# Twelve dot products of the third tile ahead of the end of the second tile's first block

## The chip, the core and the metric

The kernel runs on one core of one Trainium2 chip. The metric is the device time of one execution in microseconds (us); three executions were timed, and one was profiled. The engines are called PE (TensorE matmuls), PEld (its weight loads), DVE (VectorE), ACT (ScalarE), POOL (GpSimd) and SP (SyncE, which here only starts transfers).

## The reference

Two transformer stages over 512 tokens of width 1024, in float32. The first block mixes tokens (a convolution and an RWKV recurrence) and then has a feed-forward part made of 16,384 single-row experts: for every token 128 experts are picked (8 heads, 16 each), and

```
ue = jnp.take(expert_u, expert, axis=0)                 # 128 rows of 1024 per token
ve = jnp.take(expert_v, expert, axis=0)
h = gelu(einsum('thkd,td->thk', ue, xc))                # 128 dot products per token
return einsum('thk,thkd->td', gate * h, ve)             # weighted sum of 128 rows
```

Its result is added to the residual stream, and an RMS norm with `final_g` ends the first block. The second block has two layers (differential attention, an MLP, latent attention, a second MLP) and a last norm. Attention in it is causal.

## The kernel before

The 512 tokens are four tiles of 128 (tile 0 to 3; the change speaks of tile 1, the second, and tile 2, the third). For each tile `peer(t)` (line 980) does the expert part in two halves. The **dots** (`dots_rows`, 942): 128 times, POOL starts a gather of 128 rows of `peer_u` (one row of 4 KB per partition, so 0.5 MB), and DVE multiplies it with the tile's activations and sums along the row (line 952). The product itself goes to a scratch tile `scr`, named `dots`, that is never read; only the sum in `hc` counts. The **mix** (`mix_pe`, 957): 128 times, POOL gathers 128 rows of `peer_v`, and PE adds them with weights into one PSUM tile `pv` (line 977); the trace holds eight records for each such row set. Below, a "row" of the mix is one such gather with its matmuls.

Gathers rotate over the buffers of `k.rings`: four with the tag `gath` and four with `gatv`, for tile 2 two more with the tags `h2` and `h3`. All gathers are issued by POOL, in one order.

`x2(t)` (987) ends the first block of a tile: it loads the residual `xq` (a `gatv` buffer) and the gain `fing` (a `gath` buffer), scales `pv` and adds (1002, 1003), writes the sum to DRAM and reads it back in row layout into `h[t]`, squares it on ACT with a row sum (1009) and finishes the norm on DVE (`rstd2`, then 1013). The squares need somewhere to go as well:

```
scr = self.gp.tile([P, D], BF16, name="dots")            # dots_rows, 949
sq = self.gp.tile([P, D], BF16, name="sqr", tag="dots")  # x2, 998
```

The pool `gp` has one buffer per tag unless more are asked for, so `scr` and `sq` are one piece of memory. A tile holds its buffer until its last access; who asks next for the same tag waits for that.

The tile framework orders each engine's instructions by itself: what comes first in the program has priority, an instruction is placed when its data and its buffers are there, and later work fills what is left. The program order around the change is: `peer(1)`; the rest of the first block for tiles 1 to 3 and the routing of tiles 2 and 3; `x2(1)`; then for tile 2 and for tile 3 `peer(t)` and `x2(t)`; then the second block, which takes tiles 0 and 1 together (attention 1154, `mlp` 1233, `mla` 1271, `mlp`), then the attention of tile 2 alone, then the attention of tile 3 alone, and last `mlp`, `mla`, `mlp` for tiles 2 and 3 together. The second block's weights come in 0.5 MB tiles that ACT and DVE split into a high and a low part (211, 212). The second block of tiles 0 and 1 needs `h[0]` and `h[1]`; the transposes at its head (`norm_T`, line 1081) take both tiles into one PSUM tile, and one ACT instruction (1086) reads the pair. So in time the second block of tiles 0 and 1 runs beside the expert part of tiles 2 and 3.

Of the kernel before, what the change touches and what calls it, by code (L numbers as in the profile page):

```python
# [145 lines left out]
class K:  # L146
# [792 lines left out]
        self.gather(g, self.A[table], col)  # L939
        return g  # L940

    def dots_rows(self, t, idx):

        nc = self.nc
        if t >= 2:
            self.u2[t] = self.gp.tile([P, D], F32, name="u2", bufs=1)
            nc.sync.dma_start(self.u2[t], self.u2d[t])
        hc = self.gp.tile([P, P], F32, name="hc", bufs=1)
        scr = self.gp.tile([P, D], BF16, name="dots")
        for s in range(P):  # L950
            g = self.row('peer_u', idx[:, s:s + 1])
            self.last_dot = nc.vector.scalar_tensor_tensor(scr, g, 1.0, self.u2[t], op0=OP.mult, op1=OP.mult, accum_out=hc[:, s:s + 1])  # L952
        return hc
# [23 lines left out]
            self.nc.tensor.matmul(ps[32 * c:32 * c + 32, q, :], self.win[k // 16 % 2][:, o:o + 32], g[:, c * 256:(c + 1) * 256],  # L977
                                  start=i == 0, stop=i == 31)

    def peer(self, t, gate, idx, idxT):  # L980

        hc = self.dots_rows(t, idx)
        self.nc.scalar.activation(hc, hc, AF.Gelu)
        self.nc.vector.tensor_tensor(hc, hc, gate, op=OP.mult)
        return self.mix_pe(hc, idxT)
# [385 lines left out]
def build(tc, A, out):  # L1371
    with ExitStack() as ctx:
        k = K(tc, A, out)
# [3 lines left out]
        with ExitStack() as c1:  # L1377
            k.s1_setup(c1)
            cdots = cpeer.enter_context(ExitStack())
            routed = k.routed  # L1380

            def peer(t):
                return k.peer(t, *routed[t])
# [35 lines left out]
            *x1, conv_in = k.s1_in(g1, act1, (1, 2, 3))  # L1419
            conv_in()  # L1420
            y = peer(0)
            x = k.gp.tile([P, D], F32, name="xo", tag="gath", bufs=NGATH)
            k.x2(0, y, x)
# [10 lines left out]
            with tc.tile_pool(name="o1", bufs=1) as o1:  # L1434
                act = act_tile(o1, 1)
                k.s1_out((mix[0][:, :, :P], None), (1,), act)
                routed[1], = k.route(act, (1,), o1)
            y = peer(1)
            rwkv(2)
            rwkv(3)  # L1440
# [1 line left out]
            k.s1_out((mix[0][:, :, P:], None), (2, 3), act)  # L1442
            routed[2], routed[3] = k.route(act, (2, 3), k.rp)
        k.b2_setup(ctx)
        k.x2(1, y, k.h[1])
        cdots.close()
        tc.nc.sync.dma_start(k.h[0], k.x2d)
        g, v = k.rings[:2]
# [1 line left out]
        rings = {2: ring + [(k.b2c, "h2", 1), (k.b2c, "h3", 1)], 3: ring + [(k.b2c, "h3", 1)]}  # L1450
        for t in (2, 3):
            k.rings = rings[t]
            y = k.peer(t, *routed[t])
            k.h[t] = k.b2c.tile([P, D], F32, name=f"h{t}")
            k.x2(t, y, k.h[t])
        pool = ctx.enter_context(tc.tile_pool(name="b2", bufs=1))
# [34 lines left out]
```

## Time and profile before

| | |
|---|---|
| time of three runs | 2903.47, 2909.51 (median), 2913.26 us |
| the profiled execution | 2908.32 us, of which the profile's span is 2906.5 |
| PE busy | 2324.7 us (80% of the span) |
| DVE busy | 2036.6 us (70%) |
| POOL busy | 1239.5 us (43%) |
| ACT busy | 936.6 us (32%) |
| gathers (POOL queue) | 536.94 of 862.51 MB moved |

Busy shares are means over stages with different limits, so the stages are read one by one below. A PE share near 1 says that matmuls follow each other, not that each runs at its best speed; PEclk is the clock that the chip granted, 1.00 for 2.4 GHz and 0.50 for 1.2 GHz.

### The profile page before, as it was taken

Reading aid. Unit: us, or ns where it says so; the run is one execution under the profiler, and the core shown is the slowest. Engines: PE = TensorE matmul, PEld = TensorE weight load, DVE = VectorE, ACT = ScalarE, POOL = GpSimd, SP = SyncE. Lnnn points to the kernel's source line nnn. Section 1 sums busy time; section 2 is a strip of 40 time slices with the busy share of each in tenths; the row PEclk is TensorE's granted clock in tenths of the full one; section 3 lists DMA queues with packets and bytes.
Section 4 is the critical chain, followed back from the end, with each engine's and each line's share of the span. In section 5 each row is a group of like instructions: output and inputs, shape, how many; then the busy total and the mean of one; then the engine's idle time right before and its main releaser. Section 6 shows DMA issues by size and latency. Waiting matters only on the chain.

```text
span 2906.5 us, 50631 instructions
## 1 busy us (share of the span) xinstructions
PE 2324.7 (80%) x19212; PEld 1673.5 (58%) x19212; DVE 2036.6 (70%) x4923; ACT 936.6 (32%) x1814; POOL 1239.5 (43%) x1072
## 2 busy tenths in 40 slices
PE   6486397889672776486699997999897589999998
PEld 5365255436551541264566665778552268887897
DVE  5938987745899980599934469999751476675566
ACT  3342131031200110143333344444450255455454
POOL 0553665664376657556654434455547100000000
PEclk9668698689766886695799998999997699999999
DMA  9558898899899999998999988899999745652564
GB/s 322 168 184 318 307 402 289 290 346 348 256 360 374 399 379 409 332 350 295 365 398 363 357 290 324 297 367 384 373 369 381 258 126 182 189 157 84 157 186 135
DMA packets 249084, 862.51 MB, mean 297 GB/s; under 512 B 27652, under 2 KB 38404, under 8 KB 248840
## 3 DMA queue, kind: packets, MB, share of 16 engines
q0 software_dynamic: 147456, 536.94, 49.6%
q1 hardware_dynamic: 98792, 318.14, 32.2%
q10 hardware_dynamic: 2592, 4.20, 0.4%
q8 instruction: 151, 2.47, 0.4%
q14 instruction: 93, 0.76, 0.1%
HBM read 851.30 MB, written 7.86 MB: 296 GB/s over the span
## 4 chain that ended last, share of the span: by engine, by line
PE 35%; DVE 12%; issue 7%; DMA 3%; ACT 2%; POOL 1%; DVEq 0%; ACTq 0%; POOLq 0%
PE acc L222 9%; PE acc L223 9%; PE acc L221 9%; DVE dots L952 4%; PE pv L977 3%; DVE wlo L212 3%; DMA gath<-in_peer_v_dram,idxT 3%; PE sc L1065 2%; PE sc L1330 1%; ACT whi L211 1%; POOL gath L932 1%; PE o_ps L1342 1%; PE aT_ps L1142 1%; PE sc L1135 0%; DVE act L1087 0%
## 5 line engine op out<-in xcount | busy, mean ns | idle before, releaser
L932 POOL DMA_INDIRECT gath<-in_peer_u_dram,idx x512 | 612.1, 1195 | 511.2 <-DVE dots L952 158.9
L932 POOL DMA_INDIRECT gath<-in_peer_v_dram,idxT x512 | 544.8, 1064 | 404.7 <-PE pv L977 278.9
L212 DVE TENSOR_TENSOR wlo<-wraw,whi 128x1024 fp32r<-128x1024 f32 (+3 forms) x406 | 484.9, 1196 | 280.4 <-ACT whi L211 277.4
L952 DVE SCALAR_TENSOR_TENSOR dots<-gath,u 128x1024 bf16<-128x1024 f32 x512 | 622.7, 1216 | 20.5 <-DMA gath<-in_peer_u_dram,idx 16.9
L211 ACT ACTIVATE whi<-wraw 128x1024 fp32r<-128x1024 f32 (+3 forms) x406 | 419.9, 1036 | 510.1 <-PE acc L223 341.5
L977 PE MATMUL pv<-gath,win 128*32 128x256 f32 x4096 | 363.6, 449 | 97.7 <-DMA gath<-in_peer_v_dram,idxT 95.1
L222 PE MATMUL acc<-wlo,act 128*128 128x512 f32 (+2 forms) x924 | 375.3, 407 | 24.9 <-DVE wlo L212 23.9
L221 PE MATMUL acc<-whi,act 128*128 128x512 f32 (+2 forms) x924 | 344.8, 403 | 22.5 <-DVE qr L1115 10.2
L223 PE MATMUL acc<-whi,act 128*128 128x512 f32 (+2 forms) x924 | 361.2, 393 | 0.9 <-DVE act L200 0.8
L221 PE MATMUL acc<-act,whi 128*128 128x256 f32 x1104 | 320.1, 291 | 12.2 <-ACT whi L211 7.8
L223 PE MATMUL acc<-act,wlo 128*128 128x256 f32 x1104 | 318.4, 291 | 7.8 <-DVE wlo L212 7.4
L222 PE MATMUL acc<-act,whi 128*128 128x256 f32 x1104 | 316.6, 287 | 0.0
L219 PE MATMUL acc<-act,wraw 128*128 128x128 f32 (+2 forms) x1472 | 293.2, 357 | 4.3 <-ACT sc L856 2.7
L977 PEld LDWEIGHTS pv<-gath,win 128*32 128x32 f32 x4096 | 96.3, 116 | 286.4 <-DMA gath<-in_peer_v_dram,idxT 206.6
L219 PEld LDWEIGHTS acc<-act,wraw 128*128 128x128 f32 x1472 | 224.4, 201 | 59.4 <-issue 3.4
L222 PEld LDWEIGHTS acc<-wlo,act 128*128 128x128 f32 x924 | 176.9, 192 | 98.1 <-DVE wlo L212 50.1
L221 PEld LDWEIGHTS acc<-act,whi 128*128 128x128 f32 x1104 | 214.5, 195 | 27.7 <-ACT whi L211 10.9
L223 PEld LDWEIGHTS acc<-act,wlo 128*128 128x128 f32 x1104 | 213.9, 195 | 24.2 <-DVE wlo L212 12.2
L222 PEld LDWEIGHTS acc<-act,whi 128*128 128x128 f32 x1104 | 215.1, 195 | 4.0 <-issue 3.3
L221 PEld LDWEIGHTS acc<-whi,act 128*128 128x128 f32 x924 | 173.5, 192 | 76.0 <-issue 20.4
L223 PEld LDWEIGHTS acc<-whi,act 128*128 128x128 f32 x924 | 176.9, 192 | 34.6 <-DVE act L247 1.5
L1002 DVE TENSOR_TENSOR pv<-pv,gt_ffn 128x512 f32<-128x512 f32 x8 | 5.6, 696 | 173.8 <-PE pv L977 173.7
(422 smaller groups left out, 3132.8 us busy)
## 6 DMA issues: line engine op xcount, KB each, us to landing
wraw<-in_w_up_dram SPq DMA_DIRECT2D x128, 512.0 KB
wraw<-in_w_down_dram SPq DMA_DIRECT2D x128, 512.0 KB
wraw<-in_w_qkv_dram SPq DMA_DIRECT2D x72, 512.0 KB
wraw<-in_ada_w_dram SPq DMA_DIRECT2D x48, 512.0 KB
wraw<-in_w_q_dram SPq DMA_DIRECT2D x48, 512.0 KB
wraw<-in_w_in_dram SPq DMA_DIRECT2D x44, 512.0 KB
wraw<-in_w_out_dram SPq DMA_DIRECT2D x24, 512.0 KB
wraw<-in_w_o_a_dram SPq DMA_DIRECT2D x24, 512.0 KB
```

What stands on the lines that cost most here:

```text
L211: self.nc.scalar.activation(hi[:, :n], raw[:, :n], AF.Copy)
L212: self.nc.vector.tensor_tensor(lo[:, :n], raw[:, :n], hi[:, :n].bitcast(F32), op=OP.subtract)
L219: mm(out, l[0], r[0], start=start, stop=stop)
L221: mm(out, l[0], r[0], start=start, stop=False)
L222: mm(out, l[0], r[1], start=False, stop=False)
L223: mm(out, l[1], r[0], start=False, stop=stop)
L932: self.nc.gpsimd.indirect_dma_start(out=out, out_offset=None, in_=table, in_offset=bass.IndirectOffsetOnAxis(ap=col, axis=0))
L952: self.last_dot = nc.vector.scalar_tensor_tensor(scr, g, 1.0, self.u2[t], op0=OP.mult, op1=OP.mult, accum_out=hc[:, s:s + 1])
L977: self.nc.tensor.matmul(ps[32 * c:32 * c + 32, q, :], self.win[k // 16 % 2][:, o:o + 32], g[:, c * 256:(c + 1) * 256], start=i == 0, stop= ...
L1065: self.nc.tensor.matmul(ps[:, t0 * P:t0 * P + n], q, kT[cs, h, :n], start=start and t0 == 0, stop=False)
L1142: self.pt_ins = nc.tensor.transpose(ps[:, b, :], p[:, b * P:(b + 1) * P], self.ident)
L1330: MM(ps[:, :nk], qrT[hs, h // 2, js], self.krT[hs, :nk], start=False, stop=False)
```

## The change

`x2(1)` is no longer called between the routing and `peer(2)`. It is handed to `peer(2)` as a function, and `dots_rows` calls it when twelve of tile 2's 128 dots stand in the program. The other 116 dots come behind it. Nothing is added to the work or taken from it.

```
-    def dots_rows(self, t, idx):
+    def dots_rows(self, t, idx, mid=None):
...
         for s in range(P):
+            if s == 12 and mid is not None:
+                mid()
             g = self.row('peer_u', idx[:, s:s + 1])
...
         k.b2_setup(ctx)
-        k.x2(1, y, k.h[1])
+        y1 = y
...
-            y = k.peer(t, *routed[t])
+            y = k.peer(t, *routed[t], (lambda: k.x2(1, y1, k.h[1])) if t == 2 else None)
```

`peer` only passes the function through.

## Rows read from the trace of the kernel before

**Rows 1.** The page, busy time, share and instructions of each engine.
```profile
PE 2324.7 (80%) x19212; PEld 1673.5 (58%) x19212; DVE 2036.6 (70%) x4923; ACT 936.6 (32%) x1814; POOL 1239.5 (43%) x1072
```

**Rows 2.** By stage: length; PE, PEld, DVE, ACT, POOL busy; clock, DMA share, GB/s.
```profile
1209.00:1432.00 223.00, 160.70 (x622) 114.77 (x620) 221.25 (x503) 77.38 (x190) 146.66 (x117) 0.75 0.94 345
1432.00:1718.00 286.00, 279.50 (x2198) 190.48 (x2199) 129.55 (x190) 98.19 (x155) 137.71 (x129) 0.99 0.97 362
1718.00:1857.00 139.00, 116.34 (x539) 88.11 (x538) 125.67 (x333) 64.25 (x150) 60.90 (x51) 0.85 0.80 279
1857.00:2064.00 207.00, 194.22 (x1172) 167.55 (x1173) 205.68 (x343) 99.76 (x155) 110.08 (x80) 0.99 0.99 368
2064.00:2198.00 134.00, 119.26 (x902) 69.09 (x904) 79.82 (x181) 58.27 (x115) 69.62 (x66) 0.97 0.97 368
2198.00:2292.00 94.00, 54.44 (x498) 11.93 (x490) 6.58 (x18) 1.90 (x6) 50.44 (x54) 0.65 0.88 337
2292.00:2402.00 110.00, 92.92 (x442) 70.46 (x440) 79.58 (x164) 62.46 (x115) 0.00 (x0) 0.89 0.54 177
2402.00:2590.00 188.00, 185.34 (x1177) 168.82 (x1176) 119.56 (x181) 93.98 (x147) 0.00 (x0) 0.99 0.59 178
2711.00:2897.00 186.00, 183.19 (x1160) 166.73 (x1160) 115.94 (x175) 92.17 (x145) 0.00 (x0) 0.99 0.54 165
```

**Rows 3.** Timeline of DVE: start, duration, line, operation, idle before it and releaser.
```profile
1181.14 0.70 DVE L1002 TENSOR_TENSOR pv<-pv,gt_ffn 128x512 f32<-128x512 f32 x1 [90.89 <-PE pv L977]
...
1194.92 0.21 DVE L192 TENSOR_SCALAR rstd_s<-x_ss 128x1 f32<-128x1 f32 x1 [10.64 <-ACT sqr L1009]
1195.05 1.21 DVE L952 SCALAR_TENSOR_TENSOR dots<-gath,u 128x1024 bf16<-128x1024 f32 x1
...
1207.77 1.41 DVE L1013 SCALAR_TENSOR_TENSOR h<-h,rsq_y,fing 128x512 f32<-128x512 f32 x2
...
1431.27 1.28 DVE L1121 TENSOR_TENSOR h<-h,acc 128x512 f32<-128x512 f32 x2
...
2197.75 0.69 DVE L1121 TENSOR_TENSOR h<-h,acc 128x512 f32<-128x512 f32 x1 [2.41 <-PE acc L223]
...
2288.15 0.21 DVE L192 TENSOR_SCALAR rstd_s<-x_ss 128x1 f32<-128x1 f32 x1 [7.41 <-ACT sqr L1009]
...
2290.80 1.41 DVE L1013 SCALAR_TENSOR_TENSOR h<-h,rsq_y,fing 128x512 f32<-128x512 f32 x2 [0.19 <-DVE rsq_y L174]
```

**Rows 4.** Timeline of ACT around the squares of tile 1.
```profile
1193.32 0.63 ACT L1009 ACTIVATE sqr<-h 128x512 bf16<-128x512 f32 x1 [55.70 <-DMA h<-xsd]
...
1194.70 0.19 ACT L1009 ACTIVATION_READ_ACCUMULATOR sqr<-h 128x1 f32 x1
```

**Rows 5.** Timeline of POOL, gathers of tile 2's dots.
```profile
1172.08 0.94 POOL L932 DMA_INDIRECT gath<-in_peer_u_dram,idx  x1 [2.93 <-DMA gath<-in_peer_v_dram,idxT]
...
1181.38 0.93 POOL L932 DMA_INDIRECT gath<-in_peer_u_dram,idx  x1 [1.38 <-PE pv L977]
...
1198.64 0.96 POOL L932 DMA_INDIRECT gath<-in_peer_u_dram,idx  x1 [0.30 <-issue]
...
1211.55 1.12 POOL L932 DMA_INDIRECT gath<-in_peer_u_dram,idx  x1 [0.30 <-issue]
```

**Rows 6.** Timeline of PE, first transposes of the second block with both tiles there.
```profile
1208.58 2.18 PE L1081 MATMUL tps<-cst,h 128*128 128x128 f32 x9 [27.50 <-DVE h L1013]
```

**Rows 7.** All gathers (line 932), time from issue to landing.
```profile
DMA to landing us min/median/max: 4.2/7.4/15.9
```

**Rows 8.** Line 952 alone by stage; two instructions make one dot.
```profile
1209.00:1432.00 223.00, 140.75 (x230) 0.75 0.94 345
1857.00:2064.00 207.00, 96.55 (x158) 0.99 0.99 368
```

**Rows 9.** Line 977 alone by stage; eight records make one row of the mix.
```profile
1432.00:1718.00 286.00, 78.49 (x1024) 21.80 (x1024) 0.99 0.97 362
2064.00:2198.00 134.00, 40.52 (x536) 12.20 (x540) 0.97 0.97 368
```

More of the change, by code (lines that the diff above doesn't have):

```diff
@@ L978, in mix_token, with peer @@
                                   start=i == 0, stop=i == 31)
-    def peer(self, t, gate, idx, idxT):
-        hc = self.dots_rows(t, idx)
+    def peer(self, t, gate, idx, idxT, mid=None):
+        hc = self.dots_rows(t, idx, mid)
         self.nc.scalar.activation(hc, hc, AF.Gelu)
```

## Prediction

> **What bounds the kernel now.** The page's busy shares come first [rows 1]: no engine is full over the span, so the bound changes from stage to stage. I then cut the span where the second block's stages end, at the last residual add of each (the first such row ends at 1432, the fifth at 2198 [rows 3]), and read busy time by stage [rows 2].
>
> Two streams run side by side from 1209 us on. The gather stream does the dots and the mix of tiles 2 and 3. The block stream does the second block of tiles 0 and 1, then the attention of tile 2. In 1209 to 1432 (attention of tiles 0 and 1) DVE is the bound, busy 221 of 223 us, 141 of it in 115 dots [rows 2, 8]. In 1432 to 1718 (first MLP beside the mix of tile 2) PE is, 280 of 286. In 1857 to 2064 (second MLP beside dots of tile 3) DVE again, 206 of 207. The block stream ends at 2198; the last mix still has 61 rows to go, and from 2198 to 2292 the block stream has nothing to do. The attention of tile 3 starts after `x2(3)`, whose last instructions start at 2290.80 [rows 3]. Behind 2292 no gathers run: 2292 to 2402 is one tile's attention, 2402 to 2590 and 2711 to 2897 are the two MLPs. These show what such stages cost alone.
>
> So now the gather stream sets the time, and the block stream has 94 us to spare. The block stream waited as well, from 1181 to 1208.58: PE idles 27.5 us until tile 1's norm is done [rows 6].
>
> **The change, step by step.** It moves no work between engines; it moves `x2(1)` behind twelve dots. Its four loads and one gain on SP's queue and its stores on SP's and ACT's go with it, behind at most the load of tile 2's activations and of `h[0]`; both are wanted no earlier than `x2(1)`'s own result. The PSUM tile `pv` is next needed by tile 2's mix, long after.
>
> The step that counts is the scratch buffer. The squares of `x2(1)` and the throw-away output of tile 2's dots are one buffer. Now the squares come first, and the dots wait for them: six gathers were issued from 1172.08 to 1181.38, a landing takes 7.4 us at the median [rows 5, 7], DVE has nothing for 10.64 us, yet the first dot starts at 1195.05, just when the second square's sum is out at 1194.89 [rows 3, 4]. After the change the dots' scratch tile is asked for first, and it is one tile for all 128 dots. So the squares have to wait for dot 128, not for dot 12. The first half of `x2(1)` runs early; its second half, `h[1]`, and with it the block stream wait for all of tile 2's dots. Behind the squares on ACT, and behind the norm on DVE, stands the second block, which needs `h[1]` anyway. The gain `fing` keeps a `gath` buffer until line 1013, so the 116 dots have nine buffers in place of ten; a gather holds one for about 0.9 to issue, 7.4 to land and 1.2 for the dot, 9.5 us, in which 7.4 gathers start at the pace below. So that costs nothing unless landings grow past 9.5 us.
>
> *Start of the block stream.* With POOL free to go, gathers start every 1.291 us (1198.64 to 1211.55 is ten steps [rows 5]), while dots of 1.21 us ran back to back. The sixth gather starts at 1181.38; 122 more take 157.5, so the last starts near 1339; 7.4 to land and 1.2 for the dot give 1347.5. Squares take 1.6 (1193.32 to 1194.89 [rows 4]); from there to the end of line 1013 it is 4.1 us without dots in between, as for tile 3 (2288.15 to 2292.21 [rows 3]). That is 1353 against 1209.2 now: **+144**. Bounds: at the dot's own 1.21 us per gather +134; at the 1.94 per dot of the shared stage (223/115) +223, which I leave to a rival because the ten steps were measured with the same dots running.
>
> The Trainium skill ("SBUF — State Buffer", "Summary: rules for kernel authors") says that a DVE instruction with two SBUF inputs and a GpSimd operation that reads SBUF block each other fully. Here the gathers between back-to-back dots took 0.96 to 1.12 us against 0.94 before any dot [rows 5], so the trace shows little of it; the rule would make the dots-only stretch longer, which is the third rival.
>
> *Attention of tiles 0 and 1 without dots.* It takes 223 us beside 115 dots. Alone: PE is busy 161 us at a granted clock of 0.75; at the 0.89 of the one-tile stage that is 136, and that stage had 17 us in which PE was not busy (110 - 93 [rows 2]). So 153, **-70**. Bounds: 121 + 17 = 138 at full clock (-85), 161 + 17 = 178 at the present clock (-45).
>
> *More mix beside the block stream.* Now 128 rows of tile 2 cost the first MLP 98 us (286 against 188 alone), 0.77 each, and 67 rows of tile 3 cost the attention of tile 2 24 us (134 against 110), 0.36 each [rows 2, 9]: 122 in all. Afterwards the mix of tile 2 starts with the block stream. At 2.1 us a row (between 134/67 = 2.0 and 286/128 = 2.2) some 102 rows fall into the attention of tiles 0 and 1; no row shows that pair, so I take 0.6 (bounds 0.36 and 0.77): 61. The other 26 cost 20 in the first MLP. Tile 3's dots move there as well, and then its mix moves to the second MLP (100 rows, 77) and the attention of tile 2 (28 rows, 10). Together 168: **+46**, bounds +21 and +63.
>
> *Dots of tile 3.* 79 of them cost the second MLP 21 us (207 against 186 [rows 2, 8]), 0.27 each. Half of them now fall into the first MLP, whose work alone is the same (188 against 186): **0**. If they slowed it by as much as a row of the mix (0.77), it would be some +30; PE, which they don't use, speaks against that.
>
> *The end.* Nothing waits for tile 3's mix any more, so the 94 us of spare time at 2198 are used up: **-94**. The block stream then goes straight into the attention of tile 3, without weights already loaded in the new pool: **+5**, bounded by 0 and by twice the 7.4 us of a landing, 15.
>
> Sum: 144 - 70 + 46 - 94 + 5 = **+31**. The profiled execution took 2908.3 (span 2906.5 and 1.8 around it), 1.2 below the median of the runs. So 2939 on its scale, and 2940 for a median.
>
> **The rivals.** *First, the relief is larger than the delay* (the other side). Same order, but the pair attention runs at full clock alone (138) and mix rows cost it 0.36. Then 144 - 85 + 21 - 94 + 0 = -14, 2896. For it: that stage's clock is 0.75 now, and DVE holds it back. Against: PE fills the MLP stages to 98%, so extra mix rows there are paid for. It decides from about 30 us less than my two terms together.
>
> *Second, the scratch buffer does not bind* and the second half of `x2(1)` follows dot 12. Then twelve dots fill the 10.64 us hole and some of the next; the gather stream, which sets the time, is ahead by at most 12 x 1.29 = 15 us, less what the later start of `x2(1)` takes: -10, 2900. For it: the block stream has 94 us to spare. Against: the first dot's wait for the squares [rows 3, 4].
>
> *Third, gathers and dots hold each other up* in the dots-only stretch, at 1.94 us a step in place of 1.29: 122 x 0.65 = 79 more, 3019. Against it are the ten steps of [rows 5].
>
> *Fourth, the change alters nothing*: the planner keeps the order. Then 2909.5. The dots have data from about 1180, so I see little room for that.
>
> **How the numbers follow.** 0.3% of this time, 9 us, is about what a measurement here can tell from no change. The forecast (held back to dot 128, a net loss) has 0.66, the first rival 0.15, the second 0.13, the third 0.04, the fourth 0.02. The unknown terms alone (clock -15 to +25, row price -25 to +17, end -5 to +10, pace -10 to +10) seldom fall on one side together; half of their sum gives 2912 to 2971 for the forecast. To leave out at most 2 in 10 the range takes in the first two rivals and a bit more above: 2896 to 2985. Slower: nearly all of the forecast, the third rival and a little of the first, 0.69. Same: 0.16, from the edges of forecast, first and second, and the fourth. Faster: 0.15, half each from the first and second.
>
> **What the profile of the changed kernel should show.** Line 1009 for tile 1 near 1348 and line 1013 ending near 1353, PE without matmuls of the second block from 1181 to there, and dots back to back in between at about 1.29 us. The mix of tile 2 beside the attention of tiles 0 and 1, which takes some 210 us. No stretch like 2198 to 2292: tile 3's mix ends before the attention of tile 2 does, and the attention of tile 3 follows at once, near 2323. The prediction is wrong if line 1009 for tile 1 stands near 1200, or if the block stream's stages from attention to attention sum to less than 930 us (now 989).

## The result and the profile after

The changed kernel takes 2941.06 us (median of four runs, 2939.96 to 2949.49) against 2906.49 before: a ratio of 1.0116, 95% interval 1.0092 to 1.014. The profiled execution took 2949.49, the longest of the four; its span is 2947.7, that is 41.2 more than the span before.

The page's first part hardly differs from [rows 1]; the work is the same, and PE's and POOL's busy times even fall a little:

```profile
PE 2293.4 (78%) x19212; PEld 1652.2 (56%) x19212; DVE 2051.8 (70%) x4923; ACT 931.0 (32%) x1814; POOL 1234.1 (42%) x1072
```

The timelines tell what happened. First ACT, with the squares of tile 1 (line 1011 now), which answer to [rows 4]; then DVE, to [rows 3]; then PE, to [rows 6]:

```profile
1362.93 0.63 ACT L1011 ACTIVATE sqr<-h 128x512 bf16<-128x512 f32 x1 [220.74 <-DVE dots L954]
...
1364.08 0.19 ACT L1011 ACTIVATION_READ_ACCUMULATOR sqr<-h 128x1 f32 x1
```

```profile
1183.24 0.70 DVE L1004 TENSOR_TENSOR pv<-pv,gt_ffn 128x512 f32<-128x512 f32 x1 [88.52 <-PE pv L979]
1183.84 1.22 DVE L954 SCALAR_TENSOR_TENSOR dots<-gath,u 128x1024 bf16<-128x1024 f32 x1
...
1361.66 1.22 DVE L954 SCALAR_TENSOR_TENSOR dots<-gath,u 128x1024 bf16<-128x1024 f32 x1
1362.82 0.08 DVE L954 DVE_READ_ACCUMULATOR dots<-gath,u 128x1 f32 x1
...
1368.17 1.42 DVE L1015 SCALAR_TENSOR_TENSOR h<-h,rsq_y,fing 128x512 f32<-128x512 f32 x2
...
2337.91 0.69 DVE L1123 TENSOR_TENSOR h<-h,acc 128x512 f32<-128x512 f32 x1 [1.52 <-PE acc L223]
```

```profile
1371.28 1.20 PE L1083 MATMUL tps<-cst,h 128*128 128x128 f32 x9
```

ACT was idle for 220.74 us before the square, since 1142, and the releaser in brackets is the last dot. Not all of that is the wait for the dots: the load of `h[1]`'s first half is issued at 1210.67 and lands 6.0 us later, so the squares had data from about 1217 on and the dots held them for some 146 us. The square starts as soon as the sum of dot 128 is read out (1362.90). Before, it was the other way round: the dot followed the square. PE's first transposes of both tiles move from 1208.58 to 1371.28.

The stages answer to [rows 2]. The first row is the stretch of the dots; then come the attention of tiles 0 and 1, first MLP, `mla`, second MLP, attention of tile 2, attention of tile 3, and the two MLPs of tiles 2 and 3 (columns as there):

```profile
1181.00:1370.00 189.00, 4.93 (x41) 1.57 (x38) 163.94 (x274) 3.54 (x9) 136.06 (x131) 0.50 1.01 386
1370.00:1560.00 190.00, 189.54 (x1358) 110.92 (x1354) 99.24 (x273) 76.51 (x196) 97.61 (x93) 1.00 0.92 339
1560.00:1784.00 224.00, 215.04 (x1454) 174.83 (x1454) 172.78 (x285) 96.89 (x152) 100.66 (x80) 0.99 0.94 342
1784.00:1930.00 146.00, 114.18 (x530) 85.78 (x530) 136.28 (x347) 61.18 (x143) 81.50 (x63) 0.81 0.87 307
1930.00:2194.00 264.00, 256.68 (x1911) 183.54 (x1911) 143.93 (x225) 99.58 (x161) 132.83 (x114) 0.99 0.96 356
2194.00:2338.00 144.00, 119.94 (x656) 75.69 (x648) 84.36 (x199) 58.82 (x115) 31.87 (x27) 0.85 0.62 224
2338.00:2447.00 109.00, 90.27 (x443) 68.17 (x443) 80.87 (x166) 62.80 (x118) 0.00 (x0) 0.95 0.56 180
2447.00:2632.00 185.00, 182.90 (x1173) 166.84 (x1173) 118.05 (x180) 92.88 (x145) 0.00 (x0) 1.00 0.58 179
...
2753.00:2938.00 185.00, 181.82 (x1160) 165.35 (x1160) 116.47 (x176) 92.57 (x146) 0.00 (x0) 1.00 0.54 166
```

The stretch with no block stream, 94 us at 2198 before, is gone: the attention of tile 3 starts where that of tile 2 ends, at 2338.6, though tile 3's own input is ready at 2291.8. In its place stand 189 us with almost no PE work at the head.

What runs beside the stages answers to [rows 8] and [rows 9]: first the dots (two instructions each), then the mix (eight records each). The pair attention has no dots and 92 rows of the mix; the first MLP has 45 dots and 34 rows; `mla` has 62 dots; the second MLP has 21 dots and 93 rows.

```profile
1181.00:1370.00 189.00, 157.72 (x256) 0.50 1.01 386
...
1560.00:1784.00 224.00, 54.97 (x90) 0.99 0.94 342
1784.00:1930.00 146.00, 75.60 (x124) 0.81 0.87 307
1930.00:2194.00 264.00, 25.67 (x42) 0.99 0.96 356
```

```profile
1370.00:1560.00 190.00, 56.06 (x736) 15.76 (x732) 1.00 0.92 339
1560.00:1784.00 224.00, 20.59 (x272) 5.78 (x272) 0.99 0.94 342
...
1930.00:2194.00 264.00, 57.47 (x744) 15.57 (x744) 0.99 0.96 356
2194.00:2338.00 144.00, 22.91 (x288) 6.17 (x280) 0.85 0.62 224
```

### The profile page after: what moved, and what is told of

The parts are those of the page before. It is cut to its first block, busy times and chain, and to the rows that moved or that the text cites. A ratio compares the mean times of both kernels' runs of the same rounds, so it can differ in the third digit from the quotient of the medians.

```text
span 2947.7 us, 50607 instructions
## 1 busy us (share of the span) xinstructions
PE 2293.4 (78%) x19212; PEld 1652.2 (56%) x19212; DVE 2051.8 (70%) x4923; ACT 931.0 (32%) x1814; POOL 1234.1 (42%) x1072
## 5 line engine op out<-in xcount | busy, mean ns | idle before, releaser
L932 POOL DMA_INDIRECT gath<-in_peer_u_dram,idx x512 | 596.0, 1164 | 454.8 <-DVE dots L954 122.0
L932 POOL DMA_INDIRECT gath<-in_peer_v_dram,idxT x512 | 555.3, 1085 | 446.1 <-PE pv L979 345.4
```

The costliest lines, as they stand in the source:

```text
L932: self.nc.gpsimd.indirect_dma_start(out=out, out_offset=None, in_=table, in_offset=bass.IndirectOffsetOnAxis(ap=col, axis=0))
```

## Experiments

The theory: the time is lost because one scratch buffer ties the squares of tile 1 to dot 128. The rival: the twelve dots in front, with the later loads of `x2(1)`, cost the time themselves. All ratios are against the kernel before on the same chip. e8, e9 and e10 ran on a chip where the kernel before takes 2971 us, so they are compared by ratio, and the stages of e8 among themselves.

**e1: the scratch tile asked for twice.** In `dots_rows`:

```
             if s == 12 and mid is not None:
                 mid()
+                scr = self.gp.tile([P, D], BF16, name="dots")
```

> The changed kernel, but the dots ask for their scratch tile a second time right behind the moved block end, so the squares can have the buffer after dot 12. If the loss comes from the shared scratch buffer (theory): squares near 1215 us, first block of tile 1 done near 1225, time 2895 to 2912, as before the change or a little less. If it comes from the twelve dots in front and the later loads of x2(1) themselves (rival): 2930 to 2945, as after the change.

Measured: 2916.43 us, ratio 1.0023 (1.0003 to 1.0043). On ACT's timeline the squares no longer wait for a dot but for their data:

```profile
1215.00 0.63 ACT L1012 ACTIVATE sqr<-h 128x512 bf16<-128x512 f32 x1 [70.70 <-DMA h<-xsd]
```

So one line that changes nothing but the life of a buffer takes away four fifths of the loss. What is left, some 7 us (1 to 12 by the interval), lies above the theory's expectation. The head start of twelve dots is lost again, because now dot 13 waits for the squares, as dot 1 did before [rows 3]:

```profile
1217.32 0.21 DVE L192 TENSOR_SCALAR rstd_s<-x_ss 128x1 f32<-128x1 f32 x1 [11.17 <-ACT sqr L1012]
1217.45 1.22 DVE L955 SCALAR_TENSOR_TENSOR dots<-gath,u 128x1024 bf16<-128x1024 f32 x1
```

The block stream starts 22 us later (1231.6 against 1209.2), which it could afford. But as it ends later, more of tile 3's mix lies beside it: 41 rows are left when it ends, where some 60 were, and the whole mix takes 233 us in place of 212. Tile 3's `pv` is read to its end only at 2292.9 (2280.0 before), and that sets the time there.

**e2: behind one dot in place of twelve.** `s == 12` becomes `s == 1`, nothing else.

> The changed kernel with the block end behind one dot in place of twelve, one scratch tile. Theory (scratch buffer): the squares still wait for dot 128, 2933 to 2948. Rival (the twelve dots themselves): a twelfth of the loss, 2906 to 2913.

Measured: 2946.86 us, ratio 1.0148 (1.0120 to 1.0175): the whole loss with a twelfth of the dots in front. ACT's row is that of the changed kernel:

```profile
1363.29 0.63 ACT L1011 ACTIVATE sqr<-h 128x512 bf16<-128x512 f32 x1 [222.86 <-DVE dots L954]
```

With e1 this settles the cause: as long as one scratch tile serves all dots, it is of no account how many stand in front; whether that tile is free decides.

**e3: the kernel before, with the squares elsewhere.** In `x2`:

```
-        sq = self.gp.tile([P, D], BF16, name="sqr", tag="dots")
+        sq = xq.rearrange("p a b -> p (a b)")
```

> The kernel before, with the squares of x2 written into the residual tile xq (free by then) and not into the shared scratch tile; no order changed by hand. Theory: tile 2's dots lose their 10.6 us wait for the squares and start near 1184; the gather stream, which sets the time before the change, ends some 10 us earlier: 2893 to 2904. Rival: the buffer is of no account, 2904 to 2910.

Measured: 2900.97 us, ratio 0.9982 (0.9967 to 0.9997). DVE's timeline shows the wait of 10.64 us gone; the first dot now follows the block end's own products at once:

```profile
1190.26 0.70 DVE L1002 TENSOR_TENSOR pv<-pv,gt_ffn 128x512 f32<-128x512 f32 x1 [93.03 <-PE pv L977]
...
1192.93 0.69 DVE L1003 TENSOR_TENSOR xq<-xq,pv 128x512 f32<-128x512 f32 x1
1193.54 1.22 DVE L952 SCALAR_TENSOR_TENSOR dots<-gath,u 128x1024 bf16<-128x1024 f32 x1
```

The shared buffer cost the kernel before about 5 us too (1 to 10 by the interval), at the median half of what the removed wait would give. The first dot doesn't start near 1184 as expected, because this execution reaches the end of tile 1's mix 9 us later than the profile of the kernel before.

**e4 and e5: hold the block end to dot 64 or dot 96.** As e1 with `s == 64` and `s == 96`: how much delay can the block stream bear?

> As e1, but the block end and the second scratch tile behind dot 64. Theory with spare time (the block stream can start late at no cost until its 94 us are used): block stream starts near 1290, gather stream ends some 20 us earlier, attention of tile 3 starts near 2272: 2880 to 2900. Rival (every held dot costs its share of the loss): half of it, 2918 to 2928.

> As e4, but behind dot 96. The block stream starts near 1335. Theory (spare time first, then loss): the block stream ends near 2300, about when the gather stream does, and the attention of tile 3 starts near 2305: 2908 to 2922. Rival (every held dot costs its share of the 35 us): 2930 to 2936.

Measured: 2908.32 us, ratio 1.0008 (0.9986 to 1.0030), and 2927.52, ratio 1.0080 (1.0051 to 1.0109). Both lie between theory and rival. The stage ends, read from the residual adds and the reads of `pv` in each timeline (us):

| | block stream starts | attention of tile 2 ends | tile 3's `pv` read | `x2(3)` ends | attention of tile 3 ends |
|---|---|---|---|---|---|
| before | 1209.2 | 2198.4 | 2280.0 | 2292.2 | 2403.3 |
| e4, dot 64 | 1289.0 | 2259.6 | 2284.9 | 2297.4 | 2406.1 |
| e5, dot 96 | 1333.2 | 2314.6 | 2281.4 | 2294.7 | 2423.3 |
| the change | 1369.6 | 2338.6 | 2269.8 | 2291.8 | 2447.1 |

The first 80 us of delay cost nothing that the runs can tell (-4 to 9 us by the interval), as the spare time says. The gain that e4 was to bring, a gather stream done 20 us earlier, didn't come: its end hardly moves (2268 to 2293 in e1 to e6 as well). The traces show where the gain goes. In e4 tile 3's dots end 41 us earlier than before (2018.0 against 2059.5), but its mix then takes 257 us in place of 212. Before, some 60 of the 128 rows ran after the block stream had ended, at 1.3 us each; in e4 only 16 do, and the others, beside the block stream, take 2.1 each. The later the block stream runs, the more rows it has beside it.

In e4 the gather stream still ends last, 38 us behind the attention of tile 2; in e5 the block stream does, by 20 us, and in the change by 47. The attention of tile 3 starts behind the later of the two. From e4 to the change 81 us more of delay cost 41 us by the profiles and 31 by the ratios, 4 to 5 for each 10.

**e6: the change with the squares elsewhere.** The edit of e3 in the changed kernel.

> The changed kernel with the squares of x2 written into the residual tile and not into the shared scratch tile. Theory: the block end runs on behind dot 12 as soon as its data are back, block stream starts near 1225: 2896 to 2912. Rival (the twelve dots themselves cost): 2930 to 2945.

Measured: 2904.56 us, ratio 0.9980 (0.9960 to 1.0000). As expected by the theory, and the same as e3 (0.9982): with the squares elsewhere, twelve dots in front cost nothing that these runs can tell.

**e7 and e8: what the stages take alone.** e7 leaves out 124 of tile 2's 128 mix rows (`if few and k % 32: continue` in `mix_pe`); e8 leaves out the same of tile 3 and 124 of its dots too.

> The changed kernel with 124 of tile 2's 128 mix rows left out (rows 0, 32, 64 and 96 stay), so that the attention of tiles 0 and 1 runs with next to nothing beside it. The sum took 153 us for that stage alone and 0.6 us for each row of the mix beside it: 153 expected, bounds 138 and 178. Rival: the stage alone is shorter than 138 and a row costs as much as in the first MLP, 0.77 (190 measured with 92 rows would give 119).

> The changed kernel with the gather stream behind tile 2's dots left out (124 of 128 mix rows of tiles 2 and 3, 124 of tile 3's 128 dots), so that the second block of tiles 0 and 1 and the attention of tile 2 run with next to nothing beside them from about 1370 us. The sum's terms: attention of tiles 0 and 1 153 us (bounds 138 and 178), first MLP 188, second MLP 186, attention of tile 2 110. Rival, by which the pair attention is shorter alone (below 138) and a mix row costs it more than 0.6 us: 115 to 135.

e7 (2888.48 us, one execution) told nothing of the pair attention alone: tile 3's dots moved into the gap, and the pair attention took 221 us beside them (1369.0 to 1589.7), as beside tile 2's. e8 (2787.76, one execution) has the block stream alone, in its stages from 1428 on:

```profile
1428.00:1593.00 165.00, 157.25 (x678) 112.10 (x675) 115.05 (x317) 81.92 (x211) 5.61 (x6) 0.85 0.43 137
1593.00:1780.00 187.00, 184.84 (x1176) 168.52 (x1174) 118.09 (x180) 92.97 (x145) 0.00 (x0) 0.99 0.55 176
1780.00:1881.00 101.00, 94.42 (x537) 76.74 (x535) 69.79 (x221) 58.67 (x143) 0.00 (x0) 0.98 0.42 127
1881.00:2067.00 186.00, 184.06 (x1174) 167.09 (x1174) 118.97 (x184) 95.62 (x153) 0.00 (x0) 1.00 0.56 182
2067.00:2283.00 216.00, 179.75 (x809) 132.66 (x809) 158.36 (x346) 118.96 (x226) 0.00 (x0) 0.91 0.50 162
```

The pair attention, with next to nothing beside it, takes 165 us, not 153, but inside its bounds, so the rival (below 138) is out; the MLPs 187 and 186, as costed; the attentions of tiles 2 and 3 216 together, 106 and 110 by their residual adds. That makes a mix row beside the pair attention cost (190 - 165)/92 = 0.27 us, and a dot beside `mla` (146 - 101)/62 = 0.73, if these stages take the same on both chips, as the MLPs do.

**e9 to e12: the squares apart and the block end held.** Squares in the residual tile, the block end behind dot 64 (e9), 32 (e10, and once more as e11) and 44 (e12).

> As e6 (squares in the residual tile), with the block end behind dot 64. If the 94 us of spare time can be used and the x2 of tile 2 no longer holds back tile 3's dots: 2885 to 2900. If the end of the gather stream stays where it was in all runs so far (pv of tile 3 read at 2270 to 2293 us): 2900 to 2912.

> As e9 with the block end behind dot 32: 2888 to 2902 by the first reading, 2898 to 2910 by the second.

> The kernel of e10 once more, to see whether it beats the kernel before on another day or chip. If the gain of e10 (0.43%) is real: a ratio of 0.993 to 0.999. If it was drift of that chip: 0.999 to 1.003.

> As e10 with the block end behind dot 44. Between e10 and e9: a ratio of 0.995 to 1.000 if the time has a flat bottom where the block stream's spare time is used up.

Ratios: dot 64 0.9979 (0.9950 to 1.0009); dot 32 0.9957 (0.9934 to 0.9979) and 0.9967 (0.9948 to 0.9986); dot 44 0.9978 (0.9960 to 0.9995). With the squares apart and the block end behind 32 dots the kernel is 0.3 to 0.4% faster than before, twice over: 2899.81 against 2907.45 us in e11. By their ratios e9 falls on the border of its two readings, e10 into the first; e11 and e12 came out as expected. The spare time, from the end of the attention of tile 2 to that of `x2(3)`, is 94 us before, 36 at dot 12 (e6), 19 and 20 at dot 32 (e10, e11), 14 at dot 44 (e12), and overdrawn by 9 at dot 64 (e9). The ratios hardly differ over this stretch: the differences between 12, 32 and 44 dots lie within their intervals, and so does that to e3, in which nothing is held (0.9982): that the hold adds to the gain of the separate buffer is not shown.

## Why the prediction was right, step by step

The mechanism was the one forecast: held to dot 128 by the scratch buffer (the squares' wait for the last dot, e1, e2), a block stream that starts late and ends last. The signs that it named came out: the squares at 1362.9 (1348 forecast), the norm done at 1369.6 (1353), no stretch without a block stream, the attention of tile 3 at once behind that of tile 2 (2338.6; 2323), and 969 us from attention to attention, above the 930 that would have spoken against it. The time, 2941 against 2940, is nearer than the terms deserve: most of them missed, by 7 to 24 us, and cancelled, which is luck. Differences after minus before in us, from the stages of the two profiles:

| term | forecast | measured |
|---|---|---|
| block stream starts later | +144 | +160 (1369.6 - 1209.2) |
| pair attention: dots out, rows in | -70 + 61 = -9 | -33 (223.3 to 190.3) |
| first MLP | -98 + 20 + tile 3's dots | -62 (285.8 to 224.2) |
| `mla` | 0 | +7 |
| second MLP | +77, less dots | +58 (206.5 to 264.4) |
| attention of tile 2 | -24 + 10 = -14 | +10 (134.4 to 144.1) |
| spare time used up | -94 | -94 |
| entry into the attention of tile 3 | +5 | -3 (111.1 to 108.5) |
| sum | +31 | +44 before rounding; the other stages -3 |

*The start, 16 us short.* The step of 1.291 us came from ten gathers. In the changed kernel ten steps inside the stretch are just as quick (1208.11 to 1220.77, 1.266 each), and that is the pace of the dots: back to back they start 1.27 us apart, their 1.22 and the read-out of the sum, so the bound of 1.21 was out of reach. The stretch as a whole took 179.1 us for 128 dots, 1.40 each; 128 x 1.27 is 162. DVE's group of the last 116 dots (busy, mean ns, idle before) shows most of the rest, 12.0 us of waiting for the landing of a gather, in 12 waits, about one for every ten dots:

```profile
L954 DVE SCALAR_TENSOR_TENSOR dots<-gath,u 128x1024 bf16<-128x1024 f32 x116 | 142.0, 1224 | 15.6 <-DMA gath<-in_peer_u_dram,idx 12.0
```

POOL's timeline, which answers to [rows 5], shows a quick run and the first stall behind it, and a later one; DVE's shows the dots beside them:

```profile
1208.11 0.98 POOL L932 DMA_INDIRECT gath<-in_peer_u_dram,idx  x1 [0.30 <-issue]
...
1220.77 0.94 POOL L932 DMA_INDIRECT gath<-in_peer_u_dram,idx  x1 [0.30 <-issue]
1222.62 1.81 POOL L932 DMA_INDIRECT gath<-in_peer_u_dram,idx  x1 [0.92 <-DVE dots L954]
...
1343.12 1.97 POOL L932 DMA_INDIRECT gath<-in_peer_u_dram,idx  x1 [0.30 <-DMA gath<-in_peer_u_dram,idx]
```

```profile
1222.40 1.23 DVE L954 SCALAR_TENSOR_TENSOR dots<-gath,u 128x1024 bf16<-128x1024 f32 x1
...
1343.06 1.23 DVE L954 SCALAR_TENSOR_TENSOR dots<-gath,u 128x1024 bf16<-128x1024 f32 x1 [1.05 <-DMA gath<-in_peer_u_dram,idx]
```

Both late issues end 2.03 us after the start of the dot in which they began. So do all: of the 120 issues from 1184 to 1355 us, 114 began while a dot ran, and all of these ended 2.03 to 2.05 us after that dot's start. An issue that begins late in a dot takes 0.95 to 0.98 us, one that begins early up to 1.97; the six that began outside a dot took 0.93 to 0.94. The dots were not held: they start 1.27 us apart beside the issues while their data are there. The prediction read 0.96 to 1.12 us and saw little of this, because the gathers of its ten steps began late in a dot, one of them outside; the gather just ahead of them, at 1196.54, took 1.80. So the mechanism of the third rival is there in one direction, a gather's issue waits for the running dot, but at a far smaller price than its 1.94 us a step: 13 issues began early enough to take more than 1 us, and all issues together took some 10 us more than 0.96 each. The Trainium skill ("SBUF — State Buffer", "Summary: rules for kernel authors") says that of a DVE operation with two SBUF inputs and a GpSimd operation that reads SBUF the second one to issue blocks until the first finishes. The trace agrees for the gathers, in all 114 cases, and not for the dots, none of which waited for an issue.

Over the stretch the DMA share is 1.01 at 386 GB/s, and 0.524 MB at that rate is 1.36 us, so by their rate the transfers alone would fill nearly the whole stretch too. Which of the two, late issues or full transfers, made the dots wait is not separated by any run.

*The pair attention, 24 us too dear.* The price of 0.6 us per row was a guess between 0.36 and 0.77; by e8 it is 0.27, under the lower bound. The stage alone takes 165, inside its bounds. Beside the rows PE ran at a granted clock of 1.00, against 0.85 alone in e8 and 0.75 beside the dots; the rows themselves are PE work, so part of their price may have come back as clock. No run held the clock fixed, so that is not shown.

*The attention of tile 2, 24 us too cheap.* It has 36 rows beside it now and 67 before, and is still 10 us longer. Its granted clock is lower now (0.85 against 0.97), but that doesn't explain it: in e7 the same stage, without rows, took 110 us at nearly the same clock (0.84):

```profile
2165.00:2275.00 110.00, 90.77 (x364) 65.20 (x362) 77.64 (x180) 55.97 (x109) 0.00 (x0) 0.84 0.44 138
```

In e8, without rows too, it took 106. In all other runs, with 35 to 68 rows beside it, it took 132 to 144, and not longer with more rows. So a price per row was the wrong form for this term: halving the rows gave nothing back. What in the stage sets its length is open.

*The MLP stages* came out as priced: 187 + 34 x 0.77 + 45 x 0.27 = 225 (224 measured), and 186 + 93 x 0.77 + 21 x 0.27 = 263 (264).

*Tile 3's dots at no cost* was wrong in one place: 62 of them beside `mla` at 0.73 each, where 49 stood before, made it 7 us longer.

Of the rivals, the second is what e1 and e6 build, and its forecast of 2900 is near their 2916 and 2905. The first (relief larger than delay) didn't come; its order of events is that of the change, and e4 shows that it breaks even only at half the delay.

## What to carry to other kernels

Before moving a step into a loop, look up which buffers both ask for: a throw-away output that shares a single buffer with the moved step ties it to the loop's last pass, wherever in the loop it stands. Judge a delay by the stream that ends last: here 80 us on the other stream were free, and each 10 of the next 81 cost 4 to 5. Ten steps can miss what comes once in ten: here they gave 1.27 to 1.29 us a gather, the whole stretch 1.40, and the transfer rate at full DMA share, 1.36, came nearer.

## What the runs showed of the hardware

The issue of a gather on POOL waits for the dot that runs on DVE: in the changed kernel all 114 issues that began within a dot ended 2.03 to 2.05 us after its start, some 0.8 after its end, and took 0.95 to 1.97 us, against 0.93 to 0.94 outside a dot. The dots did not wait for the issues.

The granted clock of one stage depended on what ran beside it: the pair attention had 1.00 beside 92 rows of the mix, 0.85 with next to nothing beside it (e8), and 0.75 beside dots. That the rows paid for part of themselves in this way is not shown.

And chips differ: the kernel before took 2971.34 us at the median on one chip and 2906 to 2909 in the other comparisons, while the MLPs without gathers took 187 and 186 us there as well. Most of the difference arises early: there tile 1's `pv` is read at 1228 to 1238 us (e8 to e10), in the other runs at 1177 to 1191.
